# Raw bf16 tokens in the latent stage: moving the norm behind the products, folding squares by adds, and list-scheduling stage 1

## The chip, the cores and the metric

The kernel runs on the eight cores of one Trainium2 chip, four on each die. Each core holds the keys of one whole sequence of 4,096 tokens and answers 1,024 queries of its own, so four cores share one of the two sequences. The metric is device time in microseconds (us), taken from the slowest of the eight cores. The kernel before takes 2765.43 us (median of 3 runs, 2764.4 to 2767.24).

Some executions fall into a slower state: the cores of one die show a lower granted TensorE clock than the others, and the run takes longer, by up to some 430 us (3197.51 at most for the kernel before). Such runs are left out. "Fast" below means a run without that.

## The reference, cut to what matters

The first stage of the block makes, for every token of the sequence, 512 key/value latents and a 64-wide rotary key from the normalised token. The latents are normalised a second time before use.

```python
def rmsnorm(x, g):
    xf = x.astype(jnp.float32)
    r = lax.rsqrt(jnp.mean(xf * xf, axis=-1, keepdims=True) + NORM_EPS)
    return (xf * r).astype(x.dtype) * g
...
        u = rmsnorm(h, ln1_g[l])
        z = u @ w_in[l]                                                 # (B, S, IN_WIDTH)
        zb, zc, zv, q_lat, kv_lat, k_rope, gates = jnp.split(z, IN_SPLIT_IDX, axis=-1)
...
        q = (rmsnorm(q_lat, q_a_g[l]) @ w_q_b[l]).reshape(b, s, N_HEADS, QK_HEAD_DIM)
        kv = (rmsnorm(kv_lat, kv_a_g[l]) @ w_kv_b[l]).reshape(b, s, N_HEADS, QK_NOPE_DIM + V_HEAD_DIM)
```

The token's norm factor r is one number per token, and the gain belongs to the contraction index. So (x r g) W = r (x (g W)). The second norm divides a common factor r out again, up to its small epsilon. Only the rotary key, which is not normalised on the spot, needs r itself.

## The kernel before: the parts that the change touches

Stage 1 works on 16 groups of 256 tokens, with the features on the partitions. `mm` is a TensorE product (line 379 in the profile before), `act` an instruction of ScalarE (L384), `stt` and `tt` are VectorE instructions with one and with no scalar (L391, L395), `cp` is a VectorE copy (L408), `dma` a transfer (L411). The sum of squares over 2,048 features is a product with a matrix of ones, 16 products for a group.

```python
    def squares(g):
        for q in range(4):
            b = (4 * g + q) % NXQ
            act(sq[:, q, :], xq[:, b, :], AF.Square, [Txq[b]], [Tsq[q]])

    def xstat(g):
        for k in range(16):
            mm(PS[BST][:, 0:GW], ones, sq[:, k // 4, (k % 4) * GW:(k % 4 + 1) * GW], k == 0, k == 15,
               [Tones, Tsq[k // 4]], [TP[BST]])
        rsq(rstdx[g % 2], PS[BST][:, 0:GW], 2048.0, [TP[BST]], [Trstdx[g % 2]])

    def make_u(g):
        ub = g % 2
        for k in range(16):
            b = (4 * g + k // 4) % NXQ
            stt(uc[ub][:, k, :], xq[:, b, (k % 4) * GW:(k % 4 + 1) * GW], G("g1", k), rstdx[g % 2],
                ALU.mult, ALU.mult, [Txq[b], Tcst, Trstdx[g % 2]], [Tuc[ub][k]])
        # ... (the own half of an even group is copied to u_own)

    def latents(g):
        # ... 80 products of wkv with uc, into five banks of PSUM
        for m in range(4):
            act(sqkv[:, m, :], PS[m][:, 0:GW], AF.Square, [TP[m]], [Tsqkv[m]])
    # ...
    for g in range(NG):
        if g + 1 < NG:
            make_u(g + 1)
        if g + 3 < NG:
            xload(g + 3)
        latents(g)
        if g + 2 < NG:
            squares(g + 2)
        kvstat(g)
        latents_out(g)
        if g + 2 < NG:
            xstat(g + 2)
        krstat(g)
        # ...
    # ... then the query latents (products of 390 columns), their norm, and only then:
    ring("B", [P4.take(3072), P4.take(2048), P4.take(3072), P4.take(2048)], [3072, 2048] * 2,
         [b for b, pl in enumerate(plan) if pl[0][0] in ("hq", "hkv")])
    # ... (these are the slots of the head weights)
```

The whole order of stage 1 is fixed by hand. Attention, after the query latents, is placed by a list scheduler.

## Time and profile before

| core 5, the slowest | us |
|---|---|
| span | 2768.0 |
| first product of group 1's latents | 68.6 |
| query latents begin (first product of 390 columns) | 264.6 |
| first product of 512 columns (keys of head 0) | 320.3 |
| first score product (456 columns) | 360.9 |
| gates begin (table load for the sigmoid) | 1308.1 |
| one steady group of stage 1 | 12.92 |
| idle TensorE: up to 264.6 / to 320.3 / to 360.9 / to 1308.1 / to the end | 67.2 / 10.4 / 3.3 / 40.7 / 20.6 |

### The profile page before, as it was taken

The page shows a single profiled execution, that of the slowest core. Times are in us where ns is not written, and L with a number is a line of the kernel's source. Part 1 is how long each engine was busy: PE and PEld are TensorE (multiplying, and loading weights), DVE is VectorE, ACT ScalarE, POOL GpSimd, SP SyncE. Part 2 cuts the span into 40 slices and gives each one's busy share as a digit, 9 for nine tenths or more (in the row PEclk, how much of TensorE's full clock was granted, in tenths as well). Part 3 has the DMA queues.
Part 4 walks back from the last instruction along what each step waited for, and adds up shares of the span by engine and source line. Part 5 has one row for each costly group of instructions (what it writes and reads, how often), then busy time and mean ns, then how long its engine had stood idle before and what let it go on. Part 6 is the DMA issues. An engine that isn't in the chain of part 4 may idle for free.

```text
span 2768.0 us, 51934 instructions; the slowest of 8 cores (2754.8 to 2768.0 us)
## 1 busy us (share of the span) xinstructions
PE 2625.8 (95%) x18722; PEld 1653.8 (60%) x18722; DVE 1636.8 (59%) x3250; ACT 891.6 (32%) x1598; POOL 171.9 (6%) x300
## 2 busy tenths in 40 slices
PE   3898899999999999999999999999999999999997
PEld 2777555555565556565666666666646646655653
DVE  5775377887887888886111112247727745753762
ACT  3554366666666656664111112320000000000000
POOL 0000000000000000000000000001110111111010
PEclk9999999999999999999999999999999999999999
DMA  9542312020212020115444447444454445444446
GB/s 230 167 154 62 60 19 45 15 41 15 41 24 41 19 41 15 35 40 124 77 72 81 73 74 177 95 74 73 69 83 77 72 70 87 73 67 84 77 82 147
DMA packets 67112, 205.64 MB, mean 74 GB/s; under 512 B 7600, under 2 KB 7856, under 8 KB 66736
## 3 DMA queue, kind: packets, MB, share of 16 engines
q0 software_dynamic: 42624, 135.94, 30.3%
q1 hardware_dynamic: 24240, 66.38, 7.3%
q8 instruction: 156, 2.56, 0.4%
q14 instruction: 92, 0.75, 0.1%
HBM read 321.34 MB, written 14.78 MB: 121 GB/s over the span
## 4 chain that ended last, share of the span: by engine, by line
PE 80%; DVE 6%; issue 5%; ACT 4%; DMA 4%; SPq 0%; DVEq 0%; ACTq 0%; POOL 0%; POOLq 0%
PE ps L379 80%; ACT arena L384 4%; DVE arena L395 4%; DMA outT<-arena 2%; DMA arena<-xg 1%; DVE arena L391 1%; DVE arena L408 1%; DMA arena<-wall 1%; SPq L411 0%; DVEq L183 0%; ACTq L183 0%; DVE arena L401 0%; DVE arena L793 0%; DVE arena L404 0%; POOL arena L411 0%
## 5 line engine op out<-in xcount | busy, mean ns | idle before, releaser
L379 PE MATMUL ps<-arena 128*128 128x390 bf16 (+8 forms) x18722 | 2625.8, 300 | 130.1 <-ACT arena L384 82.6
L379 PEld LDWEIGHTS ps<-arena 128*128 128x128 bf16 x18722 | 1653.8, 98 | 1101.5 <-issue 253.6
L395 DVE TENSOR_TENSOR arena<-ps,arena 128x390 f32<-128x390 f32 (+6 forms) x760 | 380.3, 508 | 827.1 <-PE ps L379 714.6
L395 DVE TENSOR_TENSOR arena<-arena 128x512 bf16<-128x512 bf16 (+20 forms) x1458 | 625.0, 474 | 95.5 <-ACT arena L384 69.4
L384 ACT ACTIVATE arena<-ps,arena 128x128 bf16<-128x128 f32 (+10 forms) x672 | 436.7, 673 | 476.4 <-PE ps L379 428.4
L384 ACT ACTIVATE arena<-arena 128x390 bf16<-128x390 f32 (+11 forms) x374 | 227.8, 636 | 899.6 <-DVE arena L391 788.5
L391 DVE SCALAR_TENSOR_TENSOR arena<-arena 128x256 bf16<-128x256 f32 (+8 forms) x583 | 419.6, 754 | 90.7 <-ACT arena L384 67.9
L384 ACT ACTIVATE arena<-ps 128x512 bf16<-128x512 f32 (+13 forms) x547 | 248.3, 473 | 374.1 <-PE ps L379 370.7
L411 POOL DMA_DIRECT2D arena<-wall x294 | 170.5, 581 | 2563.4 <-PE ps L379 2322.6
L408 DVE CAST arena<-ps 128x512 bf16<-128x512 f32 x128 | 87.9, 687 | 42.1 <-PE ps L379 41.0
L404 DVE TENSOR_SCALAR arena<-arena 128x1024 f32<-128x1024 f32 (+1 forms) x90 | 72.3, 803 | 2.6 <-ACT arena L384 2.5
L391 DVE SCALAR_TENSOR_TENSOR arena<-ps,arena 128x256 bf16<-128x256 f32 x64 | 26.5, 476 | 53.2 <-ACT arena L384 53.2
L408 DVE COPY arena<-ps 128x456 f32<-128x456 f32 (+2 forms) x64 | 27.1, 423 | 1.2 <-PE ps L379 0.3
L401 DVE TENSOR_SCALAR arena<-arena 128x390 f32<-128x390 f32 (+7 forms) x36 | 20.5, 570 | 8.6 <-DMA arena<-arena 5.4
L384 ACT ACT_TABLE_LOAD x5 | 6.4, 1283 | 35.0 <-DVE arena L401 16.5
L395 DVE TENSOR_TENSOR arena<-arena,ps 128x390 bf16<-128x390 f32 (+1 forms) x24 | 12.3, 511 | 2.7 <-PE ps L379 1.2
L408 DVE COPY arena<-arena 128x6 f32<-128x6 f32 (+2 forms) x32 | 9.4, 292 | 2.0
L560 DVE MEMSET arena<- 64x4096 bf16 x1 | 3.5, 3472 | 0.9 <-issue 0.9
L408 DVE CAST arena<-arena 128x1028 f32<-128x1028 int32 (+1 forms) x5 | 3.5, 696 | 0.6 <-DMA arena<-posg 0.2
L793 DVE MEMSET arena<- 64x1040 bf16 x2 | 1.9, 925 | 0.4 <-issue 0.4
L559 DVE MEMSET arena<- 128x128 bf16 x1 | 0.2, 165 | 1.2 <-PEq L291 1.2
L411 POOL DMA_DIRECT2D arena<-wkvin x1 | 0.7, 662 | 0.9 <-POOLq L291 0.9
(7 smaller groups left out, 1.6 us busy)
## 6 DMA issues: line engine op xcount, KB each, us to landing
arena<-wall POOLq DMA_DIRECT2D x182, 512.0 KB, 5.3
arena<-xg SPq DMA_DIRECT2D x64, 512.0 KB, 5.0
arena<-wall POOLq DMA_DIRECT2D x64, 352.0 KB, 5.1
arena<-xo SPq DMA_DIRECT2D x16, 520.0 KB, 22.2
arena<-wall POOLq DMA_DIRECT2D x32, 256.0 KB, 3.8
outT<-arena SPq DMA_DIRECT2D x32, 256.0 KB, 2.6
arena<-wall POOLq DMA_DIRECT2D x16, 384.0 KB, 4.6
att_d<-arena SPq DMA_DIRECT2D x16, 260.0 KB, 2.1
```

What stands on the lines that cost most here:

```text
L379: S.add(PE, lambda e: e.matmul(out, lhsT=lhsT, rhs=rhs, start=start, stop=stop), reads, writes, cost=max(width(rhs) / 2400.0, 0.055) + 0.003)
L384: S.add(ACT, lambda e: e.activation(out=out, in_=in_, func=func, **kw), reads, writes, cost=c)
L391: S.add(DVE, lambda e: e.scalar_tensor_tensor(out=out, in0=in0, scalar=scalar, in1=in1, op0=op0, op1=op1), reads, writes, cost=dcost(out, ...
L395: S.add(DVE, lambda e: e.tensor_tensor(out=out, in0=in0, in1=in1, op=op), reads, writes, cost=dcost(out, in0, in1))
L401: S.add(DVE, lambda e: e.tensor_scalar(out=out, in0=in0, scalar1=s1, scalar2=None, op0=op0), reads, writes, cost=c)
L404: S.add(DVE, lambda e: e.tensor_scalar(out=out, in0=in0, scalar1=s1, scalar2=s2, op0=op0, op1=op1), reads, writes, cost=c)
L408: S.add(DVE, lambda e: e.tensor_copy(out=out, in_=in_), reads, writes, cost=dcost(out, in_))
L411: S.add(eng, lambda e: e.dma_start(out=out, in_=in_), reads=reads, writes=writes, chan=chan, cost=2.0)
L559: S.add(DVE, lambda e: e.memset(ones, 1.0), writes=[Tones])
L560: S.add(DVE, lambda e: e.memset(krope[64:128, :], 0.0), writes=Tkr)
L793: S.add(DVE, lambda e, i_=i_: e.memset(Qr[i_][64:128, :], 0.0), writes=[TQr[i_]])
```

## The change

The intent is fourfold. (1) The products run on raw tokens, loaded as bf16 by a casting transfer; the gain is multiplied into the weights once, r only into the rotary key, and r's epsilon is carried into the second norm. (2) Squares are folded from 2,048 to 512 columns by VectorE adds in bf16, so 4 products with ones remain of 16. (3) A core's own blocks, which the queries need in fp32 and normalised, are loaded as fp32, cast on ScalarE and normalised on VectorE apart from the latents. (4) One list scheduler now places stage 1, query latents and attention with other estimated delays, and products of attention may start before the queries are normalised. Two things come with it: the weights, one load before, come in sixteen, and the rotary table goes out to memory and back.

The diff cut to its core (lines beginning `# ...` mark cuts):

```diff
+    def wscale(k):
+        act(wkv[:, k, :], wst[k % 8], AF.Copy, [Twst[k % 8], Tcst], [Twk[k]], scale=C("g1", k))
+        if k < 8:
+            wload(k + 8)
# ...
+    def squares(g, h):
+        x, Tx = xtile(g)
+        v = sqv[:, h, :]
+        act(v, x[:, h, :, :].rearrange("p k n -> p (k n)"), AF.Square, Tx[h], [Tsqh[h]])
+        tt(v[:, 0:1024], v[:, 0:1024], v[:, 1024:2048], ALU.add, [Tsqh[h]], [Tsqh[h]])
+        tt(xs[:, g % 2, 512 * h:512 * h + 512], v[:, 0:512], v[:, 512:1024], ALU.add, [Tsqh[h]], [Txs[g % 2]])
# ...
     def xstat(g):
-        for k in range(16):
-            mm(PS[BST][:, 0:GW], ones, sq[:, k // 4, (k % 4) * GW:(k % 4 + 1) * GW], k == 0, k == 15,
-               [Tones, Tsq[k // 4]], [TP[BST]])
+        for c in range(4):
+            v = xs[:, x, :].rearrange("p (h c n) -> p h c n", h=2, n=128)[:, :, c, :]
+            mm(PS[7][:, 0:GW], ones, v, c == 0, c == 3, [Tones, Txs[x]], [TP[7]])
+        rsq(rstdx[:, y, :], PS[7][:, 0:GW], 2048.0, [TP[7]], [Trstdx[y]])
+        act(epsx[:, x, :], PS[7][:, 0:GW], AF.Copy, [TP[7]], [Tepsx[x]], scale=EPS / 2048.0, bias=EPS * EPS)
+    def own(i):
+        for k in range(16):
+            stt(u_own[:, k, o:o + 128], xo_[i % 3][:, k, :], C("g1", k), rstdx[:, y, 0:128], ALU.mult, ALU.mult,
+                [Txo[i % 3], Tcst, Trstdx[y]], [Tu[k]])
# ... latents: the products now read the raw tokens
+            mm(lps(g, m), wkv[:, k, m * 128:(m + 1) * 128], x[:, :, k, :], k == 0, k == 15,
+               [Twk[k], Tx[0][k // 4], Tx[1][k // 4]], [TP[LB(g, m)]])
# ... the loads at the start: eight slots for weights, tokens of group 0 in pieces
+    for k in range(8):
+        wload(k)
+        if k % 2:
+            for h in range(2):
+                xpiece(0, h, 4 * (k // 2), 4)
# ... group 1's tokens wait for the 14th weight (slot 5's second load)
+            f_g.units.append(Unit(lambda: xload(1, [Twst[5]]), 0.0, pos=-9.0, ok=lambda: at("w") >= 8))
# ... attention's units: keys no longer wait for the query norm, queries and values do
+        okv = lambda: F.at("pv") >= 32 * (h - 1) - 1 and F.at("b") >= h - 2 and F.at("qn") >= 0
+        okq = lambda: okk() and F.at("qn") >= 0
```

## The prediction

> **What bounds the kernel now.** I read the page's head and slice rows first, to see which engine is full and where it is not.
>
> ```profile
> span 2768.0 us, 51934 instructions; the slowest of 8 cores (2754.8 to 2768.0 us)
> ...
> PE 2625.8 (95%) x18722; PEld 1653.8 (60%) x18722; DVE 1636.8 (59%) x3250; ACT 891.6 (32%) x1598; POOL 171.9 (6%) x300
> ...
> PE   3898899999999999999999999999999999999997
> PEld 2777555555565556565666666666646646655653
> ```
>
> TensorE (PE) is the bound nearly everywhere. Only the first slice (69 us) has it at 3 tenths. The change rewrites stage 1 (the key/value latents of 16 groups of 256 tokens) and the seam behind it, all inside the first 350 us, so I then took the busy times of each engine in stretches there (columns: stretch, length, PE, weight loads, DVE, ACT, POOL, granted clock, DMA share, GB/s).
>
> ```profile
> 30.00:40.00 10.00, 2.02 (x8) 0.88 (x8) 0.00 (x0) 2.10 (x3) 0.00 (x0) 1.00 0.99 240
> 40.00:50.00 10.00, 4.81 (x21) 2.41 (x22) 5.87 (x15) 6.58 (x8) 0.00 (x0) 1.00 1.02 283
> ...
> 60.00:70.00 10.00, 5.83 (x37) 3.27 (x35) 9.99 (x23) 6.75 (x13) 0.00 (x0) 0.88 0.74 234
> 70.00:80.00 10.00, 10.00 (x74) 8.03 (x72) 8.01 (x20) 2.47 (x6) 0.00 (x0) 0.78 0.78 231
> ...
> 180.00:200.00 20.00, 18.72 (x170) 15.97 (x168) 16.50 (x43) 9.95 (x19) 0.00 (x0) 1.00 0.49 158
> ...
> 300.00:320.00 20.00, 9.92 (x71) 6.62 (x68) 5.56 (x12) 6.72 (x16) 3.17 (x6) 0.83 0.54 95
> ```
>
> Three things show. Up to 50 us the DMA engines are full and PE waits for data. From 60 to 70 DVE is full (normalising a whole group into bf16) and PE waits for it. At 300 to 320 PE is idle half the time, in the seam between the query latents and attention. In between, at 180 to 200, PE is at 94%: PE bound with small gaps. The timeline of one steady group shows what the gaps are (start, us, engine, what, idle before).
>
> ```profile
> 159.37 3.88 ACT L384 ACTIVATE arena<-arena 128x1024 bf16<-128x1024 f32 x4
> ...
> 162.45 0.60 PE L379 MATMUL ps<-arena 128*128 128x256 bf16 x4 [0.35 <-ACT arena L384]
> ...
> 163.40 0.60 PE L379 MATMUL ps<-arena 128*128 128x256 bf16 x4 [0.35 <-ACT arena L384]
> ...
> 164.45 9.76 PE L379 MATMUL ps<-arena 128*128 128x1 bf16 x87 [0.45 <-ACT arena L384]
> ...
> 167.19 6.41 DVE L391 SCALAR_TENSOR_TENSOR arena<-arena 128x256 bf16<-128x256 f32 x16
> ```
>
> ACT squares a quarter of a group in about 0.97 us; PE multiplies it by ones in 0.60 and waits 0.35 for the next. The same chain of waits repeats at 172.05 and 184.97, so one group takes **12.92 us**, of which 11.64 are PE busy.
>
> **What the Trainium skill says.** "TensorE: Matmul & The Clock Gate", Part 1: the PE clock falls to half after an idle window of about 3.4 us and comes back after as long a busy one. The trace agrees: in 2 us windows the granted clock is 0.50 from 68 to 74 us, after the idle time at 60 to 68, and 0.50 to 0.60 from 320 to 324, after an idle of 9.8 us. The same page (the matmul gap) gives N/2.4 GHz plus 2.5 ns, 109 ns for 256 columns; the trace has 64 in 7.16 us, 112 ns, which I use. "VectorE: DVE Perf Modes", Mode 2x_1P: a tensor_tensor on packed bf16 makes two results a cycle, fp32 one. The trace agrees: 419 ns for 128x512 bf16, 690 ns for 128x520 fp32. "DMA: Bandwidth & Descriptors", SWDGE vs HWDGE vs iDMA: a cast in a DMA needs the POOL queue; that is where the changed kernel puts its bf16 token loads, and the own blocks, wanted in fp32 too, load uncast. "SBUF — State Buffer", two separate sides: a DVE instruction using both ports blocks POOL's descriptor writing. No row here shows that cleanly.
>
> **The change, part by part.** The groups by form (84 to 242 us) give the prices: count, busy us, mean ns.
>
> ```profile
> L391 DVE SCALAR_TENSOR_TENSOR arena<-arena 128x256 bf16<-128x256 f32 x192 | 77.0, 477 | 0.0
> L384 ACT ACTIVATE arena<-arena 128x1024 bf16<-128x1024 f32 x48 | 46.6, 1046 | 0.0
> L391 DVE SCALAR_TENSOR_TENSOR arena<-ps,arena 128x256 bf16<-128x256 f32 x49 | 20.4, 477 | 43.5 <-ACT arena L384 43.5
> L384 ACT ACTIVATE arena<-ps 128x256 bf16<-128x256 f32 x48 | 18.4, 384 | 70.4 <-PE ps L379 70.4
> ```
>
> *(a) Steady groups.* PE before: 80 latent products, 16 ones products, 4 more for the latents' own norm, 2 tiny ones. The change keeps all but 12 of the 16: 88 x 0.112 + 0.19 = 10.05 us. The norm no longer stands ahead of the latents (they run on raw tokens; the factor falls out of the kv norm and is multiplied only into the rotary key), so the squares' wait can hide.
> Do the others fit in 10.05? DVE in a group with an own block: folding adds 2 x (0.61 + 0.34) = 1.9 (1024 and 512 bf16, scaled from the 419 ns at two a cycle); 16 own-block products of 128 columns, about 0.27 each (0.40 busy for 256, less 128 cycles at 0.96 GHz) = 4.3; four latent outputs 1.6; rotary part 1.5; the rest 0.6: **9.9 us**, against 9.3 now. Without an own block (8 of 16) it is 5.6. ACT with an own block: squares of 2 x 2048 in 2 x 1.81 (0.97 for 1024 plus 1024 more at 0.82 ns), casts 2 x 0.97, squares of latents 2 x 0.58, two Ln/Exp pairs 1.6, copies and small squares 0.8: **9.1 us**. So PE stays the bound, but with DVE at 98% and ACT at 91% in the eight own groups. Three buffers let own-block work lag, so I allow 0.25 us a group: 10.3.
> Before, group 1's latents begin at 68.6 and the last group ends at 264.6: 195.9 us for 15 groups. After: 15 x 10.3 = 154.5, plus 2 for the last group's exposed norm: 156.5. Saved: **39.4**.
>
> *(b) Start.* Before, the first 48 us move 10.04 MB into SBUF, 3.81 MB of it halved by casting, so 13.85 MB of source: 289 GB/s. Among it are 2.1 MB of later weights. After, PE takes the first group k by k as weights arrive; scaling the weights by the gain (16 of 640 columns, 0.75 each, 12 us), two sines and two halves of squares share ACT, and the second sine waits for DVE's angle table, which ends near 23 us, so weight 15 is ready near 33 and group 0 ends near 39. Group 1 also needs its tokens. Bytes ahead of it: positions and constants 1.0, two groups 4.2, weights 5.24, rotary table out and a quarter back 1.6, an own block 1.05 MB: 13.1 MB at 289 to 304 GB/s is 43 to 45 us. I take 43 for the start of group 1 (the last to arrive shares the queues), against 68.6. Saved: **25.6**.
>
> *(c) Seam.* The query latents themselves (44.95 us) do not change. After them:
>
> ```profile
> 310.03 2.64 POOL L411 DMA_DIRECT2D arena<-wall x5 [6.98 <-PE ps L379]
> ...
> 320.35 4.22 PE L379 MATMUL ps<-arena 128*128 128x512 bf16 x25 [9.63 <-DMA arena<-wall]
> ```
>
> The head weights are issued only at 310, behind loads that wait for ring slots, and PE stands 9.63 us. From 309.5 to 330 PE misses 12.7 us in all, and half clock costs 1.4 more. In the changed order the head weights stand on POOL's queue behind four query weights only, and the key products of head 0 and some convolution products fill the wait for the query norm. I take 11 of 14.1 as **saved**.
>
> *(d) Attention.* From 345 to 1250 PE is busy 867.4 of 905.0. The work is the same; the scheduler's delays are new (longer after PE, shorter overheads on ACT). Of 37.6 us idle I credit **4**, with 10 either way.
>
> Sum: 39.4 + 25.6 + 11 + 4 = 80. 2765.4 - 80 = **2685 us**. From 1250 us on (FFN, output) nothing changes.
>
> **Rivals.** *DVE or ACT becomes the bound.* DVE at 98% in eight groups leaves nothing for waits; in-order queues make PE wait for a latent output behind own-block products. If those groups took 11.5 us, 10 us are lost: 2695. Against it: the lag may last three groups and the last six have slack. *DMA takes the place of DVE at the start.* A group is 2.1 MB; at 300 GB/s that is 7 us of 10, so the loads barely get ahead; with DVE's two-port instructions delaying POOL's descriptors, group 1 might start at 55: 2697. *The gain is hidden anyway*: the page's only 95% PE says little could come, and if the norm chain were hidden already only 15 x 12 ones products (20 us) would go: 2745. Against it: PE's idle time up to 70 us and at 310. *Attention gives it back*: convolution products used early are no longer there as filler; 10 to 15 us lost.
>
> **Range and chances.** Steady groups could give 25 to 43, the start 15 to 32, the seam 7 to 14, attention -8 to 14. Taken together, not all at one end: 55 to 100 saved, or 2665 to 2710. Over 2% faster needs 2711 or less, a saving of 54: 0.91. Within 2%: 0.08. Slower: 0.01.
>
> **What would show it.** Right: 256-column products before the query latents down by 180; one steady group at 10 to 10.6 us; query latents beginning near 200 instead of 264.6; no DMA wait ahead of the first 512-column products; PE idle from then to 1250 near 35. Wrong: groups above 11 us with DVE or ACT named ahead of PE; DMA named after 45 us; a clock of 0.5 inside stage 1 after the start; more PE idle in attention than 38 us.

## More of the kernel before

The prediction shows most of the lines that matter. Two more, first the group of 256-column products up to 268 us (columns: line, engine, operation, shapes, count, then busy us, mean ns, then idle time ahead of them with its releasers), then the waits of TensorE in the first 69 us (total us, times, longest).

```profile
L379 PE MATMUL ps<-arena 128*128 128x256 bf16 x1600 | 194.0, 280 | 56.6 <-ACT arena L384 53.1 <-DVE arena L391 1.8
```

```profile
PE ps L379 <- ACT arena L384: 44.5, 12, 28.7
```

Stage 1 issues 1,600 products of 256 columns, 100 for a group: 80 for the latents, 16 for the sum of squares, 4 for the latents' own norm. Nearly all of TensorE's idle time ahead of them is a wait for ScalarE's squares, most of it before 69 us. (ScalarE waits there in its turn, 10.7 us of it for the tokens.)

## The result, and the profile after

The changed kernel's runs with the result took 2699.43 and 2699.46 us, and 2744.61 and 3044.45 in the slow state (median of all four 2722.03; the kernel before 2766.34). Two more executions, both fast, took 2702.48 and 2698.61. The ratio of the fast runs is **0.9762**, with a 95% interval of 0.9743 to 0.9782: faster by 2.4%, 66 us. Ratios here are the mean time of one kernel's fast runs over that of the other's of the same rounds, so they are not quite the ratio of the medians quoted beside them.

The profile taken with the result fell into the slow state on two cores, so I read a second one of the same kernel, taken later (`after_again` below: 2691.28 to 2703.7 us in five fast runs, ratio 0.9754 [0.9735, 0.9774]). All its cores stand at a mean clock of 0.994 to 0.997, and its slowest core is again core 5. In this kernel `mm` is L509, `act` L516, `stt` L523, `tt` L527, `cp` L540 and `dma` L543. First the head of the page.

```profile
span 2702.1 us, 51305 instructions; the slowest of 8 cores (2688.0 to 2702.1 us)
...
PE 2597.9 (96%) x18530; PEld 1637.4 (61%) x18530; DVE 1607.4 (59%) x3214; ACT 920.9 (34%) x1588; POOL 191.5 (7%) x330
...
PE   4999999999999999999999999999999999999996
```

TensorE has 192 products fewer (18,530 for 18,722) and 27.9 us less busy time. The rest of the 65.9 us between the two slowest cores is idle time. The first slice is still at 4 tenths. The table cuts both spans at the same events.

| core 5 | before | after | saved | predicted |
|---|---|---|---|---|
| to group 1's first latent product | 68.6 | 54.3 | 14.3 | 25.6 |
| from there to the query latents (15 groups) | 196.0 | 152.8 | 43.2 | 39.4 |
| query latents to the gates | 1043.5 | 1030.4 | 13.1 | 15 |
| gates to the end | 1459.9 | 1464.6 | -4.7 | 0 |
| sum | 2768.0 | 2702.1 | 65.9 | 80 |

The last row but one lies within the spread of the cores: from 1457.4 to 1466.4 us on the eight cores of this one run. The same 256-column group, up to 210 us, then answers to the line shown of before:

```profile
L509 PE MATMUL ps<-arena 128*128 128x256 bf16 x1408 | 165.5, 280 | 37.4 <-ACT arena L516 34.0 <-DMA arena<-xg 2.0 <-DVE arena L527 0.6
```

There are 1,408 products, 88 for a group, and the idle time ahead of them is 37.4 us for 56.6. All but a few us of that is at the start. The stretches (same columns as in the prediction: stretch, length, PE, weight loads, DVE, ACT, POOL, clock, DMA share, GB/s) show where.

```profile
40.00:50.00 10.00, 5.98 (x29) 3.67 (x28) 1.54 (x3) 5.87 (x8) 5.63 (x5) 1.00 0.81 141
50.00:60.00 10.00, 7.99 (x74) 6.93 (x73) 3.30 (x7) 6.84 (x10) 0.00 (x0) 1.00 1.02 217
60.00:70.00 10.00, 7.28 (x82) 6.35 (x80) 6.00 (x15) 7.72 (x11) 0.53 (x1) 1.00 1.02 244
...
120.00:140.00 20.00, 20.00 (x188) 17.92 (x187) 19.56 (x60) 16.63 (x25) 2.12 (x4) 1.00 0.47 134
140.00:160.00 20.00, 20.00 (x189) 17.90 (x188) 19.77 (x61) 17.09 (x26) 3.23 (x7) 1.00 0.92 159
...
180.00:200.00 20.00, 20.00 (x189) 17.93 (x187) 11.23 (x27) 10.58 (x20) 1.06 (x2) 1.00 0.57 109
```

From 120 us on TensorE has no gap at all, and VectorE is at 98 to 99% up to 160 us, while the own blocks are normalised. Six steady groups take 58.0 us, from 116.7 to 174.7, so one takes **9.67 us**, 110 ns for each of its 88 products (its two one-column products included). From 40 to 70 us the DMA engines are at 81 to 102% and TensorE waits. The timeline of TensorE and of the queue that issues the tokens (start, us, engine, what, idle before) shows group 1 begin:

```profile
42.15 2.12 POOL L543 DMA_DIRECT2D arena<-xg  x4 [35.55 <-DMA arena<-wkvin]
```

```profile
54.29 12.00 PE L509 MATMUL ps<-arena 128*128 128x256 bf16 x110 [2.01 <-DMA arena<-xg]
```

The tokens of group 1 are asked for at 42.15, when the 14th weight is there, and the products wait 2.01 us for them at 54.29. Group 0's own products ended only at 52.3. At the seam behind stage 1:

```profile
239.76 26.45 PE L509 MATMUL ps<-arena 128*128 128x390 bf16 x194
266.42 8.31 PE L509 MATMUL ps<-arena 128*128 128x512 bf16 x56 [0.22 <-DVE arena L527]
```

The 9.63 us ahead of the first 512-column products are gone: idle time from the query latents to the first of them is 10.4 us before and 0.0 after, from there to the first score product 3.3 and 0.7, from the scores to the gates 40.7 and 39.1. The score stretch itself is shorter, 923.2 for 947.2 us, because products that had filled it stand in the seam now (62.2 for 40.5 us between the first 512-column and the first score product).

### The profile page after: what moved, and what is told of

It reads as the page before. It is cut to its first block, busy times and chain, and to the rows that moved or that the text cites. A ratio compares the mean times of both kernels' runs of the same rounds, so it can differ in the third digit from the quotient of the medians.

```text
span 2743.0 us, 51305 instructions; the slowest of 8 cores (2688.2 to 2743.0 us)
## 1 busy us (share of the span) xinstructions
PE 2642.4 (96%) x18530; PEld 1659.0 (60%) x18530; DVE 1611.1 (59%) x3214; ACT 923.1 (34%) x1588; POOL 191.4 (7%) x330
## 4 chain that ended last, share of the span: by engine, by line
PE 85%; DVE 5%; ACT 3%; DMA 3%; issue 3%; SPq 0%; DVEq 0%; ACTq 0%; POOLq 0%
PE ps L509 85%; ACT arena L516 3%; DVE arena L527 3%; DMA outT<-arena 2%; DMA arena<-wkvin 1%; DVE arena L540 1%; DVE arena L523 1%; SPq L543 0%; DMA arena<-wall 0%; DVEq L196 0%; ACTq L196 0%; DVE arena L533 0%; DVE arena L536 0%; SPq L196 0%; ACT L516 0%
## 5 line engine op out<-in xcount | busy, mean ns | idle before, releaser
L509 PE MATMUL ps<-arena 128*128 128x390 bf16 (+9 forms) x18530 | 2642.4, 304 | 85.3 <-ACT arena L516 36.5
L509 PEld LDWEIGHTS ps<-arena 128*128 128x128 bf16 x18530 | 1659.0, 99 | 1068.3 <-issue 206.5
L527 DVE TENSOR_TENSOR arena<-ps,arena 128x390 f32<-128x390 f32 (+6 forms) x744 | 374.3, 510 | 843.6 <-PE ps L509 735.0
L527 DVE TENSOR_TENSOR arena<-arena 128x130 bf16<-128x130 bf16 (+22 forms) x1522 | 667.7, 479 | 140.7 <-ACT arena L516 108.0
L516 ACT ACTIVATE arena<-ps,arena 128x910 bf16<-128x910 f32 (+10 forms) x672 | 439.1, 673 | 486.5 <-PE ps L509 436.3
L516 ACT ACTIVATE arena<-arena 128x390 bf16<-128x390 f32 (+13 forms) x412 | 267.8, 674 | 912.9 <-DVE arena L523 796.6
L523 DVE SCALAR_TENSOR_TENSOR arena<-arena 128x1024 f32<-128x1024 f32 (+9 forms) x499 | 372.0, 761 | 34.3 <-ACT arena L516 8.5
L543 POOL DMA_DIRECT2D arena<-wall x294 | 171.1, 583 | 2362.8 <-PE ps L509 2303.5
L516 ACT ACTIVATE arena<-ps 128x512 bf16<-128x512 f32 (+12 forms) x499 | 236.4, 495 | 296.1 <-PE ps L509 290.3
L540 DVE CAST arena<-ps 128x512 bf16<-128x512 f32 x128 | 87.7, 685 | 68.6 <-PE ps L509 67.5
L523 DVE SCALAR_TENSOR_TENSOR arena<-ps,arena 128x256 bf16<-128x256 f32 (+1 forms) x80 | 33.3, 467 | 21.1 <-PE ps L509 13.4
L540 DVE COPY arena<-ps 128x456 f32<-128x456 f32 (+2 forms) x64 | 27.2, 424 | 8.0 <-PE ps L509 7.5
L543 POOL DMA_DIRECT2D arena<-xg x30 | 16.0, 549 | 153.7 <-ACT arena L516 59.5
L533 DVE TENSOR_SCALAR arena<-arena 128x390 f32<-128x390 f32 (+2 forms) x29 | 16.2, 560 | 2.3 <-DMA arena<-cst 0.7
L527 DVE TENSOR_TENSOR arena<-arena,ps 128x390 bf16<-128x390 f32 (+1 forms) x24 | 12.3, 514 | 3.0 <-PE ps L509 1.8
L540 DVE CAST arena<-arena 128x1028 f32<-128x1028 int32 (+1 forms) x5 | 3.6, 714 | 4.7 <-DMA arena<-posg 4.3
L540 DVE COPY arena<-arena 128x6 f32<-128x6 f32 (+1 forms) x24 | 3.8, 160 | 1.2
```

The costliest lines, as they stand in the source:

```text
L509: S.add(PE, lambda e: e.matmul(out, lhsT=lhsT, rhs=rhs, start=start, stop=stop), reads, writes, cost=max(width(rhs) / 2400.0, 0.055) + 0.003)
L516: S.add(ACT, lambda e: e.activation(out=out, in_=in_, func=func, **kw), reads, writes, cost=c)
L523: S.add(DVE, lambda e: e.scalar_tensor_tensor(out=out, in0=in0, scalar=scalar, in1=in1, op0=op0, op1=op1), reads, writes, cost=dcost(out, ...
L527: S.add(DVE, lambda e: e.tensor_tensor(out=out, in0=in0, in1=in1, op=op), reads, writes, cost=dcost(out, in0, in1))
L533: S.add(DVE, lambda e: e.tensor_scalar(out=out, in0=in0, scalar1=s1, scalar2=None, op0=op0), reads, writes, cost=c)
L540: S.add(DVE, lambda e: e.tensor_copy(out=out, in_=in_), reads, writes, cost=dcost(out, in_))
```

## The experiments

Four questions were open. Does TensorE or VectorE bound a steady group? What bounds the start? Would the fold alone, or the early weights alone, have done the same? Does the changed scheduling pay in attention? My theory: the groups are bound by TensorE, with VectorE on the edge; the start by bytes. The rivals: VectorE bounds the own groups; the start is bound by the slots, the gate or the order of ScalarE's work.

### e1_unfold: the changed kernel without the fold

```diff
-        tt(v[:, 0:1024], v[:, 0:1024], v[:, 1024:2048], ALU.add, [Tsqh[h]], [Tsqh[h]])
-        tt(xs[:, g % 2, 512 * h:512 * h + 512], v[:, 0:512], v[:, 512:1024], ALU.add, [Tsqh[h]], [Txs[g % 2]])
# ...
-        for c in range(4):
-            v = xs[:, x, :].rearrange("p (h c n) -> p h c n", h=2, n=128)[:, :, c, :]
-            mm(PS[7][:, 0:GW], ones, v, c == 0, c == 3, [Tones, Txs[x]], [TP[7]])
+        for c in range(16):
+            v = sqv.rearrange("p h (c n) -> p h c n", n=128)[:, :, c, :]
+            mm(PS[7][:, 0:GW], ones, v, c == 0, c == 15, [Tones] + Tsqh, [TP[7]])
```

> The changed kernel with the folding adds taken out and 16 ones products a group again instead of 4. If TensorE bounds the steady groups: 12 more products of 0.112 us in 15 groups, 20 us slower than the changed kernel (2699 to 2719), one steady group 11.4 us instead of 10.1. Rival, VectorE bounds the own-block groups: taking 1.9 us of adds away from it there gives back what the products cost, so only the other 7 groups pay, 8 to 11 us slower.

Measured: 2739.2 us median of 8 runs, four of the five fast ones between 2723.0 and 2725.8; ratio 0.9854 [0.9835, 0.9873]. The fifth took 2752.58, with one die at a clock of 0.981; it stands in the ratio, and is the profiled one, so I read core 0 of the other die. A steady group takes 10.97 us there, 1.30 more, which is 12 products at 108 ns. A stretch with own blocks on core 0:

```profile
120.00:140.00 20.00, 20.00 (x189) 17.94 (x187) 14.47 (x50) 16.80 (x24) 1.06 (x2) 1.00 0.56 152
```

TensorE stays at 20.00 of 20 with VectorE at 72%, so taking adds from VectorE and giving products to TensorE costs the full price of the products, in the groups with an own block too. **TensorE bounds the steady group.** That makes 15 x 1.3 = 20 us. The loss is some 25 us in the four undisturbed runs; the rest lies at the start: with its single buffer of squares TensorE waits 7.74 us for ScalarE at 59.4 on core 0, and the clock stands at 0.5 for 6.8 us there. (On core 0, 7.2 us are lost when group 1 ends and 23.2 when stage 1 ends.) The run also splits the gain: without the fold the rest of the change still saves some 41 us of the 66.

### e2_nogate: group 1's tokens not held behind the weights

```diff
-            f_g.units.append(Unit(lambda: xload(1, [Twst[5]]), 0.0, pos=-9.0, ok=lambda: at("w") >= 8))
+            f_g.units.append(Unit(lambda: xload(1), 0.0, pos=-9.0))
```

> The changed kernel with group 1's token loads issued at once, not behind the fourteenth weight load. In the changed kernel they were issued at 42.3 us and landed at 53.7, as group 0 ended (53.1). If the gate makes the start late, group 1's tokens land earlier but group 0 still ends near 53, so at most 1 us is gained. If bandwidth makes it late, the tokens take it from the weights, group 0 ends 3 to 6 us later, and the whole is 0 to 6 us slower.

Measured: 2713.01 us, ratio 0.9811 [0.9795, 0.9826]: 13 us worse than the changed kernel. Group 0 ends later on most cores (its last small products at 65.2, 65.9, 63.4 and 65.3 us on cores 0, 2, 4 and 7, for 65.3, 58.1, 58.6 and 58.5 in after_again), since its weights now share the queues with the tokens, and group 1 gains nothing (74.3 to 76.9 us for 72.4 to 79.9). The larger loss comes a hundred us later. Core 5 from 140 us:

```profile
140.00:150.00 10.00, 8.69 (x82) 7.68 (x80) 9.93 (x31) 8.84 (x12) 1.05 (x2) 1.00 1.04 185
150.00:160.00 10.00, 2.63 (x14) 1.44 (x12) 9.88 (x30) 9.18 (x12) 0.59 (x2) 0.65 0.69 120
```

TensorE stands for 7.4 of 10 us while VectorE is at 99%. In the changed kernel VectorE is at 99% in this stretch too, and TensorE at 100%. VectorE's lack of slack may be the cause, or something else in the shifted order; the next run tells.

### e8_own8: e2_nogate with half of VectorE's own-block work

```diff
-        for k in range(16):
+        for k in range(8):
             stt(u_own[:, k, o:o + 128], xo_[i % 3][:, k, :], C("g1", k), rstdx[:, y, 0:128], ALU.mult, ALU.mult,
                 [Txo[i % 3], Tcst, Trstdx[y]], [Tu[k]])
+        cp(u_own[:, 8:16, o:o + 128], xo_[i % 3][:, 8:16, :], [Txo[i % 3]], Tu[8:16])
```

The result is wrong: half of the own tokens' features are not normalised. (These tokens have a mean square near one and gains near one, so the comparison with the reference passed all the same.)

> The ungated kernel (2713 us, with 12 us of TensorE stall at 147 to 159 us behind a VectorE that is 99% busy) with half of the own-block products replaced by one copy of raw tokens, 1.5 us less VectorE work in each of eight groups; its result is wrong on purpose. If VectorE's lack of slack made the stall, it goes or shrinks below 3 us: about 2701. If the order of loads on the POOL queue made it, it stays: about 2712.

Measured: 2703.07 us, ratio 0.9771 [0.9754, 0.9788], against 0.9811 with the full work. Core 5:

```profile
140.00:150.00 10.00, 10.00 (x96) 8.96 (x94) 9.64 (x28) 8.04 (x12) 1.05 (x2) 1.00 1.01 175
150.00:160.00 10.00, 10.00 (x96) 8.96 (x94) 8.07 (x20) 8.45 (x14) 4.23 (x8) 1.00 0.91 147
```

The stall is gone. VectorE's missing slack made it, with one reserve: the list scheduler places each version afresh, so the order may differ a little too. The rival "VectorE becomes the bound" is real, and the changed kernel passes it by a hair.

### e3_wcast: all 16 weights asked for at once, cast by the transfer

```diff
-        dma(SP, wst[k % 8], wkvin[:, k * 640:(k + 1) * 640], "wst%d" % (k % 8), writes=[Twst[k % 8]])
+        dma(POOL, wkv[:, k, :], wkvin[:, k * 640:(k + 1) * 640], "wst%d" % k, writes=[Twk[k]])
# ... scaled in place, no slots; the eight later loads are no longer held back
```

> The changed kernel with the key/value weights loaded by casting DMA straight into their bf16 place on the POOL queue, all 16 issued at once and scaled in place: no eight staging slots to wait for, no place behind the rotary table on the SP queue. If slots and queue order pace the weights (DMA engines only 0.2 to 0.4 busy near 40 us), group 0 ends at 42 to 46 instead of 53 and the kernel is 7 to 11 us faster, about 2690. If raw bandwidth is the limit (about 240 GB/s of source), group 0 ends at 50 or later and 0 to 3 us are gained.

Measured: 2706.73 us (fast runs 2702.88 to 2706.91), ratio 0.9783 [0.9766, 0.9799]. The query latents begin at 211.4 to 213.5 us on cores 0, 2, 4 and 7, for 202.8 to 210.0 in the changed kernel. Taking the eight slots away does not help. The run is no clean test of the slots, though: the hold on group 1's tokens goes with them, so these are asked for at 17 us and share the queues with the weights, as in e2_nogate. It does give a rate for sixteen casting loads. Core 5 from 6 to 60 us:

```profile
DMA packets 5013, 9.49 MB, mean 176 GB/s; under 512 B 597, under 2 KB 3759, under 8 KB 4817
...
q0 software_dynamic: 4125, 5.85, 83.8%
```

### e5_chunk: four large weight loads instead of sixteen

```diff
+        dma(POOL, wkv[:, k:k + 4, :].rearrange("p a b -> p (a b)"), wkvin[:, k * 640:(k + 4) * 640], "wst%d" % k,
+            writes=Twk[k:k + 4])
# ... group 0's tokens in two pieces per half instead of four
```

> The changed kernel with the key/value weights cast by DMA into place in 4 loads of 10 KB a partition instead of 16 of 2.5 KB, and group 0's tokens in pieces twice as wide; no staging, no gate. The start moved about 13 MB of source by 54 us, 245 GB/s, in packets of 1 to 2.5 KB; the kernel before moved 13.9 MB in 48 us, 289 GB/s, mostly in packets of 4 KB and more. If packet size sets the rate, group 0 ends at 42 to 48 us instead of 53 and the kernel is 5 to 10 us faster than the changed one, about 2692. If the rate is the same for any packet, coarser pieces only delay the first products: 0 to 5 us slower.

Measured: 2698.36 us (fast runs 2692.42 to 2699.12), ratio 0.9739 [0.972, 0.9758]. The traffic of core 5 from 6 to 60 us, in the changed kernel and then here (a casting transfer counts half of what it reads; I take all of `q0` as casting):

```profile
DMA packets 4654, 10.77 MB, mean 200 GB/s; under 512 B 558, under 2 KB 1657, under 8 KB 4523
...
q0 software_dynamic: 1696, 2.82, 39.8%
```

```profile
DMA packets 2763, 9.89 MB, mean 183 GB/s; under 512 B 350, under 2 KB 478, under 8 KB 2511
...
q0 software_dynamic: 1806, 5.77, 77.8%
```

Read from memory are 10.77 + 2.82 = 13.59 MB in 54 us, 252 GB/s, in the changed kernel, and 9.89 + 5.77 = 15.66 MB, 290 GB/s, here, with larger pieces and 41% fewer packets. (The kernel before, with one load for all weights: 12.88 + 3.56 = 16.44 MB, 304 GB/s.) On core 5 group 1 then begins at 46.08 us instead of 54.29. The cores differ, though: in the changed kernel cores 2, 4 and 7 read at 278 to 290 GB/s and cores 0 and 5 at 246 and 252. **The size of the pieces is not what sets the rate.** By the same count e3_wcast, with sixteen loads and more packets than the changed kernel, reads 9.49 + 5.85 = 15.34 MB, 284 GB/s, on core 5 and 284 to 294 on cores 0, 2, 4 and 7, as fast as e5_chunk (278 to 290). From 10 to 36 us, with the DMA engines at 98% or more in all three, the changed kernel reads 251 to 279 GB/s on these five cores in 3,007 to 3,255 packets, e3_wcast 273 to 295 in as many, and e5_chunk 279 to 292 in 1,150 to 1,229. What sets cores 0 and 5 of the changed kernel apart is a hole: from 36 to 42 us their DMA engines are at 0.52 and 0.48, those of cores 2, 4 and 7 at 0.85 to 0.89.

Where the trace names the wait for group 1's tokens in both runs (cores 0, 2 and 5), they are ready at 48.1 us on average instead of 53.7. Of this lead of 5.6 us 3.7 are left when group 3 ends and 2.9 at the query latents; with cores 4 and 7 it is 1.3 (204.0 for 205.3). It is a lead of cores 0 and 5 alone, the two with the hole; cores 2, 4 and 7 begin the query latents 0.4 to 2.7 us later than in the changed kernel. The gain of about 0.2% in the time lies inside the intervals.

### e9_late and e6_late: the sines and the mask after the weights

Here ScalarE makes the two sines of the rotary table after the last weight instead of between the weights, and the mask loads behind group 2's tokens; e6_late puts the same on top of e5_chunk. The changed kernel ran beside them on the same chip as after_again.

```diff
-        if k in (5, 9):
-            f_w.units.append(Unit(lambda k=k: sine(k // 9), 0.0, pos=-9.0, ok=lambda k=k: F1.at("ang") >= k // 9))
         f_w.units.append(Unit(lambda k=k: wscale(k), 0.0, pos=-9.0))
+    for k in range(2):
+        f_w.units.append(Unit(lambda k=k: sine(k), 0.0, pos=-9.0, ok=lambda k=k: F1.at("ang") >= k))
```

> The changed kernel again, beside the two below on the same chip: 2698 to 2703 us in fast runs, a ratio of 0.976; group 1 begins near 54 us.

> The changed kernel with both sines, and so the rotary table's trip through memory (1 MB out, half a MB back before group 1), behind the last weight, and the 0.27 MB mask behind group 2's tokens. If the bytes ahead of group 1 set its start at about 245 GB/s, 1.3 to 1.9 MB less is 5 to 8 us less: group 1 begins near 47 us, the kernel takes about 2693. If the staging slots and queue order pace it, the table never was in the way but for 2 us of sines on ScalarE: 0 to 2 us.

> The same move of sines and mask on the version with weights in four casting loads (2692 to 2699 us): by the bytes 5 to 8 us less, about 2689, faster than both kernels; if ScalarE's in-order queue or VectorE's own-block work then stalls TensorE inside stage 1, no gain.

Measured: after_again 2700.73 us, ratio 0.9754; e9_late 2705.54 (fast runs 2697.55 to 2705.54), ratio 0.9761 [0.9745, 0.9777]; e6_late 2715.76 over six runs, three of them slow (the fast ones 2696.3 to 2698.24), ratio 0.9753 [0.9736, 0.9769]. No gain, though the start came as the bytes said: in e9_late group 1's tokens have landed at 41.9 to 46.8 us on cores 0, 2, 4, 5 and 7, for 47.7 to 57.3 in after_again. On core 5 10.65 MB had been read when group 1 began, at 236 GB/s from zero, for 12.72 MB at 234 in after_again: fewer bytes at the same rate. TensorE's timeline on core 5 of e9_late shows where the lead went:

```profile
45.08 3.65 PE L509 MATMUL ps<-arena 128*128 128x256 bf16 x32 [0.88 <-DMA arena<-xg]
51.19 6.32 PE L509 MATMUL ps<-arena 128*128 128x256 bf16 x58 [2.46 <-DVE arena L527]
61.74 1.01 PE L509 MATMUL ps<-arena 128*128 128x256 bf16 x4 [4.23 <-DVE arena L540]
...
67.94 5.34 PE L509 MATMUL ps<-arena 128*128 128x256 bf16 x48 [4.24 <-ACT arena L516]
```

Group 1 does begin 9 us earlier, at 45.08. Then TensorE waits three times, 10.9 us in all, because the rotary table and the first own block come late: they stand on one queue, behind the sines, and the own block is asked for at 58.2 us instead of 45.6. VectorE is named waiting 2.7 us for the table in the same stretch. The sines' old place was not idle cost; it was the head of another chain.

### e4_oldlag: attention placed with the old delays

```diff
+OLD = [False]
# ... lag() and the costs of ScalarE and VectorE return the old values while OLD[0] is set
     F1.go()
+    OLD[0] = True
```

> The changed kernel with attention list-scheduled by the delays and ScalarE costs of the kernel before; stage 1 and the seam's structure are as changed. If the new delays gave attention nothing (TensorE idle from the first scores to the gates was 40 us before and after), within 3 us of the changed kernel. If they gave the 4 us that I had credited, or more, 4 to 10 us slower.

Measured: 2701.8 us, ratio 0.9772 [0.9756, 0.9788]. From the query latents to the gates the cores take 1031.3 to 1035.1 us (cores 0, 2, 4 and 7) for 1026.4 to 1029.2 (the same cores of after_again). The new delays are worth some 5 us in the traces (4 to 10 were expected) and 2 to 3 in the mean of the fast runs, where the intervals overlap: small, and of the sign that I credited.

### b1_fold: the kernel before, with the fold alone

```diff
+    def fold():
+        tt(sq[:, 0, :], sq[:, 0, :], sq[:, 1, :], ALU.add, [Tsq[0], Tsq[1]], [Tsq[0]])
+        tt(sq[:, 2, :], sq[:, 2, :], sq[:, 3, :], ALU.add, [Tsq[2], Tsq[3]], [Tsq[2]])
+        tt(sq[:, 0, :], sq[:, 0, :], sq[:, 2, :], ALU.add, [Tsq[0], Tsq[2]], [Tsq[0]])
     def xstat(g):
-        for k in range(16):
-            mm(PS[BST][:, 0:GW], ones, sq[:, k // 4, (k % 4) * GW:(k % 4 + 1) * GW], k == 0, k == 15,
-               [Tones, Tsq[k // 4]], [TP[BST]])
+        fold()
+        for k in range(4):
+            mm(PS[BST][:, 0:GW], ones, sq[:, 0, k * GW:(k + 1) * GW], k == 0, k == 3, [Tones, Tsq[0]], [TP[BST]])
```

> The kernel before with one part of the change alone: squares folded by three bf16 adds of 1024 on VectorE, 4 ones products instead of 16. By counting TensorE work: 12 products of 0.112 us less in 15 groups, 20 us faster than before. By the chain of waits: the norm stands ahead of the latents, the products only filled the time in which ScalarE squared (0.97 us a quarter), and now the adds stand behind the last square, so each group gets 1 to 2.5 us longer: 15 to 35 us slower than before. The fold would then pay only with the tokens unnormalised.

Measured: 2871.93 us, ratio 1.0365 [1.0329, 1.0401]: **104 us slower**, three to seven times what I expected. TensorE's timeline and two stretches of core 5:

```profile
222.87 12.42 PE L379 MATMUL ps<-arena 128*128 128x256 bf16 x90 [8.05 <-DVE arena L395]
243.34 12.43 PE L379 MATMUL ps<-arena 128*128 128x256 bf16 x90 [8.05 <-DVE arena L395]
```

```profile
220.00:222.00 2.00, 0.00 (x0) 0.00 (x0) 1.83 (x4) 0.00 (x0) 0.00 (x0) 0.50 0.00 0
...
226.00:228.00 2.00, 2.00 (x12) 1.38 (x11) 2.00 (x6) 0.39 (x1) 0.00 (x0) 0.50 0.18 18
...
230.00:232.00 2.00, 2.00 (x21) 1.79 (x19) 1.40 (x4) 0.48 (x2) 0.00 (x0) 1.00 0.88 240
```

The period is 20.47 us instead of 12.92. The adds stand in VectorE's queue behind the latents' output and the rotary key of the group before, the ones products wait for the adds, and in this fixed order everything else of TensorE waits behind them: 8.05 us without a product in every group. A gap of that length also drops the clock to 0.50, and the first half of the next group runs at half speed: 90 products take 12.42 us, where 90 at 109 ns would take 9.8. Here, then, the fold pays only where the norm is off TensorE's path; another place for the adds in VectorE's order was not tried.

### b2_early: the kernel before, with head weights asked for early

```diff
+    rbo = A3 + 16384 + 4 * 2080
+    ring("B", [rbo, rbo + 3072, rbo + 5120, rbo + 8192], [3072, 2048] * 2,
+         [b for b, pl in enumerate(plan) if pl[0][0] in ("hq", "hkv")])
     pend = []
     for i in range(6):          # the query latents
# ... and not after them
```

> The kernel before with the head weights' slots made, and so their loads queued, ahead of the query latents; nothing else. If the 9 to 12 us of DMA wait in the seam were only the late issue: 8 to 11 us faster than before. If the wait for the query norm takes its place (the normalising products on VectorE end 15 us after the latents): 2 to 6 us faster, the rest becoming a wait for VectorE.

Measured: 2769.11 us against 2768.23, ratio 0.9987 [0.9947, 1.0026]: nothing, where even the second expectation had 2 to 6 us. TensorE's timeline on core 2:

```profile
308.63 2.04 PE L379 MATMUL ps<-arena 128*128 128x260 bf16 x21 [0.80 <-ACT arena L384]
313.89 0.31 PE L379 MATMUL ps<-arena 128*128 128x348 bf16 x1 [3.21 <-DVE arena L391]
315.74 0.45 PE L379 MATMUL ps<-arena 128*128 128x348 bf16 x1 [1.55 <-DVE arena L391]
```

The wait for the weights is gone (0.8 us idle up to the first 512-column product for 10.4), and 12.3 us of waits (3.3 before), nearly all for VectorE's query norm, stand in its place, with the clock at half for 17.1 us. So the seam's gain in the changed kernel needs products that depend on neither: keys and convolution. How much of the 13 us is due to the fill and how much to the early weights in its presence stays open.

## Why the prediction was right or wrong, point by point

The time lies within the range, 14 us above the 2685. The sum predicted was 80; measured were 65.9 on the slowest cores. That it came so near is in part luck: the groups gave 3.8 us more than predicted and the start 11.3 less.

- **(a) Steady groups: right, a term too small.** Predicted 10.3 us a group and 39.4 saved; measured 9.67 and 43.2. The mis-sized term is the product: 112 ns came from 64 products in 7.16 us, a run that includes the end of the last product; in an unbroken stream it is 109 to 110 ns, which is what the page cited there says. The allowance of 0.25 us for waits was not needed either. What those two gave was partly taken by gaps in groups 1 to 4, where TensorE waits 4.7 us in all. VectorE at 98% and ScalarE at 91% came out: 98 to 99% from 120 to 160 us, and 83 to 96% in the stretches of 20 us from 100 to 180. But VectorE's sum behind the 98% is too small. An add of 1,024 takes 0.685 us and one of 512 0.418, so the fold costs 2.2 a group and not 1.9 (the 419 ns quoted for 512 already contradict the 0.34 used); the own products take 0.29 each, the rotary part 1.8. With these an own group is 10.9 us of VectorE work against 9.67 of TensorE. TensorE stayed full because the buffers let VectorE fall behind and catch up: no rotary part is finished between 138.3 and 157.2 us, four are between 157.2 and 166.2, and VectorE is at 79% from 160 to 180.
- **(b) Start: the step that failed.** "13.1 MB at 289 to 304 GB/s is 43 to 45 us." Group 1 began at 54.3. By then this core had read 10.32 + 2.40 = 12.7 MB, so the byte count was about right, and the rate was 234 GB/s counted from zero (231 on core 0, and 253 and 254 on cores 2 and 7, each at its own start of group 1). I carried a rate over from another kernel's traffic. Why it is lower here stays open: sixteen weight loads in place of one do not explain it (e3_wcast). What the trace of core 5 shows is the hole from 36 to 42 us. In it both queues wait, the one with group 1's tokens for the 14th weight until 42.15, the other for the rotary table's way out to memory until 41.05; the prediction had no such wait. The second half of the miss, "weight 15 is ready near 33 and group 0 ends near 39", has a cause of its own besides: the last weight landed at 43.25, but was scaled only from 46.0 to 46.8, because group 0's norm and a table load stood ahead of it on ScalarE, and group 0 ended at 52.3. Saved: 14.3, not 25.6. And e5_chunk and e9_late show that a lead of group 1 is not kept whole: part or all of it is spent again by groups 2 and 3, in e9_late on the table and the first own block.
- **(c) Seam: right.** 13.0 us of idle time went, for 11 predicted, and by both means named there; b2_early shows that the first means without the second is worth nothing.
- **(d) Attention: nearly nothing.** Idle time from scores to gates fell by 1.6 us, for 4 with a doubt of 10.
- **The rivals.** DMA did take VectorE's place at the start, as the second rival had it (group 1 at 55: 2697); that VectorE delays the writing of descriptors, its reason, is shown by no run here. Attention did not give the gain back: with the old delays (e4_oldlag) TensorE idles 40.3 to 47.3 us from scores to gates on cores 0, 2, 4 and 7, and before the change 40.1 to 45.2. VectorE as the bound did not show in the changed kernel but is one shifted load away (e2_nogate, e8_own8). The gain was not hidden: the 15 groups gave 43.2 us, over twice the price of the products removed from them (15 x 12 x 0.109 = 19.6); the rest is the wait for the squares, now off the path. The count of products fell by 192, not 180, because group 0 and all others lose 12.
- **The signs.** Of those named as wrong, two came: DMA is named ahead of TensorE at 54.29, and the clock is at half for 3.4 us between 70 and 80 us (0.83 in the mean). A third, over 38 us of idle time in attention, hangs on the cut: it is 39.1 from the scores to the gates, where it was 40.7 before. A group of 9.67 us lies below the 10 to 10.6 named as right. On the clock the prediction reads its trace too freely: the longest gap between products from 60 to 69 us was 1.80 us, not 3.4, and the clock was halved all the same; in the changed kernel it was halved behind one of 2.72 us, at 69.01.

## What to carry to other kernels

Before pricing an operation that you move to another engine, ask who waits for its result: a fold by adds cost 104 us where the products wait for it, and where they do not it saved some 25. A transfer rate carried over from another kernel is a guess: ask whether each queue will have something to move at every moment, or stands behind a wait. Then ask what the next two buffers still lack, because an earlier start is soon spent if they come no earlier. When a stretch shows one engine at 100% and its neighbour at 99%, treat a change in the timing of loads as a risk.

## What the Trainium skill lacked or had wrong

- "TensorE: Matmul & The Clock Gate", the warning on the peak-current limiter in Part 1: it has a die go to 13/16 of the clock once three of its cores run dense products, and advises to budget that for all-core kernels. Here eight cores with TensorE at 96% ran at a mean clock of 0.993 to 0.998 in every fast run of the changed kernel. A clock of 0.81 did show, in some executions only: on core 0 of the profile taken with the result, 0.81 from 160 to 320 us and 0.98 from 340 to 440, with TensorE 99 and 95% busy. What sets it off stays open.
- "DMA: Bandwidth & Descriptors", Bandwidth, and "HBM Reference", Specifications: 341 GB/s for 1 MB pieces on one core, 358 as the share of a core in a pair. With all eight cores loading I counted, from 6 to 60 us, 304 to 309 GB/s in the kernel before, 278 to 290 in e5_chunk, 284 to 294 in e3_wcast (their DMA engines at 99% or more), and 246 to 290 in the changed kernel, whose queues are not always full. Neither page has a figure for all eight cores loading pieces of mixed sizes, which is what a kernel's start does.
- The matmul gap of the first page was right to the nanosecond (109 ns for 256 columns) where my own reading of the trace was 3 ns off. Its clock gate agrees for long gaps: one of 8.05 us in every group of b1_fold brought half clock each time. What the page lacks is how little work still counts as idle: the clock was halved with no gap over 1.80 us in the kernel before, and behind one of 2.72 us in the changed kernel.
